# Mixer A of both groups in one pipeline with a new order of the projection blocks, and a prefix that transposes x in two halves

## The chip, the core and the metric

One core of a Trainium2 chip. Its engines are called TensorE (PE), VectorE (DVE), ScalarE (ACT), GpSimd (POOL) and SyncE (SP), which issues nearly all of the DMAs. The metric is the device time of one execution in microseconds; every time is counted from the first instruction of the execution unless it says otherwise.

## The reference, cut to what matters

A step through two layers of a hybrid backbone, for 128 context tokens and 1024 latent tokens, with width 1024. The change lies in the even layer, ahead of its recurrence:

```python
def even_layer(x, shift, scale, gate, ...):
    h = rms_norm(x, norm_pre) * (1.0 + scale) + shift      # shift, scale = silu(c) @ ada_w + ada_b
    qa, ka, va, ga, pb, gb = split_cols(h @ w_in, ...)
    # mixer A: 8 query heads in 2 groups of 4, one key/value head each
    #   context tokens: softmax over the context tokens, with a sink
    #   latent tokens, in blocks of 128: softmax over 128 cached keys and the blocks t-1, t, t+1
    ya = gqa_context(qa, ka, va, sink) or gqa_window_latent(rope(qa), rope(ka), va, k_ctx, v_ctx, sink)
    yb = rwkv_mix(pb, state, ...)                          # mixer B: a scan over the tokens
    y = concat([ya * silu(ga), yb * silu(gb)]) @ w_out
    return x + gate * rms_norm(y, norm_post)
```

The second, odd layer (differential attention) comes after all that the change touches. All products are made from values split into two parts, `hi` and `lo`, with three matmuls for one: hi x hi, hi x lo, lo x hi.

## The kernel before

The 1152 tokens are 9 tiles of 128 (`NT`): tile 0 holds the context tokens, 1 to 8 the latent ones. The normalized and modulated x lies transposed in `hh` and `hl` (width in 8 blocks, `KT`, by 1152 tokens), in SBUF, until the end of the stage that is called the first here.

**Prefix** (in `hybrid_step`, from L675). `mod_chunks` loads four chunks of 512 columns of `ada_w`, two loads of 1 MB each in a ring of four buffers, and makes 16 rows of shift and scale of them: 8 matmuls, a copy, a transpose and a VectorE instruction for each (L289 to L303). The chunks 0 and 1 are the shift of the blocks 0 to 3 and 4 to 7, the chunks 2 and 3 the scale. Then x is loaded in three thirds of three tiles, and `normed` scales the rows (L324 to L334). `modulated` (L336) takes 3 thirds x 8 blocks: three transposes into one PSUM bank (L342), ScalarE's scale and shift into `hf` (L345), VectorE's cast into `hh` (L347) and its residual into `hl` (L348). The modulation rows and the transposes share one pool of four PSUM banks.

**Two streams of work** follow, zipped step by step by `run`. `transposed` goes through 21 blocks of 128 output columns, each in three thirds of 384 tokens (`proj_T`, 24 matmuls a third, L368 to L370): `a` and `g` blocks are gates (`gate_T`, with `silu2`, stored to `gaT` or `pbT`), `b` blocks are the inputs of mixer B (`b_block`: the padded row `bo`, the sum of the neighbours `bs` on GpSimd at L472, the mix `bm`, stored to `pbT`). Of the b blocks 4 to 7 (the keys) the squares go to `bs`, `norms` (L493) sums them by matmuls, spreads the result to `yb` (L498), and `scale` transposes `yb` (L508) and multiplies `bm` by it (L512), both put off by some steps through the list `later`. `bs` and `bm` have one buffer each. The weights of each block are loaded to `raw` (two buffers), rounded on ScalarE and their rest taken on GpSimd (L261 to L263).

The other stream is mixer A, one generator `a_group` for each of the two groups, one after the other. At step k it projects tile k (`project`, L354 to L356, rotary factors on VectorE and GpSimd), sums up the values of tile k - 2 (`values`: transposes of the probabilities at L632, value matmuls at L643 to L645, store at L652), turns tile k (`turn`) and makes the probabilities of tile k - 1 in two rounds of two heads (`probs`: score matmuls at L601, masks at L604, maximum at L608, exponentials at L614). The scores have one PSUM tile of two banks. The keys `kst`, the values `vh` and `vl` and the group's weights `wah`, `wal` have one buffer each and are allocated anew for the second group.

**The order on the engines** of all this, and of the first pieces of the RWKV stage (up to item -1 of its loop), is made by a scheduler that simulates the time (`tc.block(schedule_with_timeline_sim=True)`): every instruction has a place in the order in which the program emits it, and of those that are ready the one with the lowest place goes first; each engine then runs its list in order. The buffers of the RWKV stage (`low`, `lora` and the operand tiles `hb`, L885 to L905) take the room of the first stage's tiles.

Of the kernel before, what the change touches and what calls it, by code (L numbers as in the profile page):

```python
# [141 lines left out]
def hybrid_step(ctx: ExitStack, tc: tile.TileContext, I, O, stop=99):  # L142
# [315 lines left out]
    def b_block(i, w, later, pool, psum, p_tr, hh, hl, ind):  # L458
# [29 lines left out]
        yb = tl(pool, [P, 2 * NT, 64], "yb", bufs=1)  # L488
# [54 lines left out]
    def a_group(g, hh, hl, wp, rp, ap, psum, rope, idb, msk):  # L543
# [6 lines left out]
        kr, vr = tl(ap, [P, P], "kr"), tl(ap, [P, 64], "vr")  # L550
        SP.dma_start(kr, I["akT"][g])
        SP.dma_start(vr, I["av"][:, g])
        stack_split(kst[:, 0:P], kr)
        dup_split(vh[:, 0], vl[:, 0], vr)
        kp, vph, vpl = (tl(ap, [P, P], n, F32R) for n in ("kp", "vph", "vpl"))
        qks, qss, prs = {}, {}, {}

        def project(t):
            ps = tl(p_pr, [P, 512], "ps")
            proj_nat(ps, hh, hl, wh, wl, t, THIRD)  # L560
            qk = qks[t] = tl(ap, [P, 5, 2, 64], "qk", bufs=2)
# [7 lines left out]
            else:  # L569
                dup_split(vh[:, t], vl[:, t], ps[:, 320:384])  # L570

        def turn(t):
            qk = qks.pop(t)
            pq, pk = tl(p_tr, [P, 512], "pt"), tl(p_tr, [P, 512], "pt")
            PE.transpose(pk[:, :P], qk[:, 4].rearrange("p o d -> p (o d)"), ident)
            stack_split(kp if t == 0 else kst[:, P * t:P * t + P], pk[:, :P])
            for r in range(4):
                PE.transpose(pq[:, P * r:P * r + P], qk[:, r].rearrange("p o d -> p (o d)"), ident)
            qs = qss[t] = tl(ap, [P, 2, 512], "qs", F32R, bufs=2)
# [3 lines left out]
        def near(t):  # L583

            if t == 0:
                return [(0, kp)], [(vph, vpl)], []
            lo, hi = max(1, t - 1), min(8, t + 1)
            kv = [(vh[:, j], vl[:, j]) for j in [0] + list(range(lo, hi + 1))]
            return ([(0, kst[:, 0:P]), (P, kst[:, P * lo:P * hi + P])], kv,
                    ([(P, 0)] if t > 1 else []) + ([(P * len(kv) - P, 1)] if t < 8 else []))  # L590

        def probs(t, hp):
            runs, kv, masks = near(t)
            nk = P * len(kv)
            qs = qss[t]
# [16 lines left out]
            p = prs[t, hp] = tl(ap, [P, 2, 512], "p", bufs=2)  # L612
# [8 lines left out]
        def values(t):  # L621
            kv = near(t)[1]
            pr = [prs.pop((t, hp)) for hp in range(2)]
# [32 lines left out]
        for k in range(NT + 2):  # L656
            if k < NT:
                project(k)
                yield
            if 2 <= k:  # L660
                yield from values(k - 2)
            if k < NT:
                turn(k)
                yield
            if 1 <= k <= NT:
# [8 lines left out]
    blk.__enter__()  # L674
    with ExitStack() as ph1:  # L675
        hp = ph1.enter_context(space("hT0", 1))
        hh, hl = tl(hp, [P, KT, TOK], "hh", F32R), tl(hp, [P, KT, TOK], "hl", F32R)
        with ExitStack() as su:
            xp = su.enter_context(space("su", 2))
            ps = su.enter_context(space("psu", 4, space=PSUM, side="right"))  # L680
            ahead = []
            for j in range(4):
                for _ in mod_chunks(0, 4 * j, 4, xp, ps, "ps", lambda: tl(xp, [P, P], "mrow"), 4, ahead):
                    pass
            ahead.pop()()
            thirds = []
            for i in range(3):
# [4 lines left out]
                normed(thirds[i], xp)  # L692
            for i in range(3):
                modulated(i, thirds[i], xp, ps, hh, hl)
# [6 lines left out]
        left, right, rope = load_cst(bp, "left", "right", "rope")  # L701
# [6 lines left out]
        for i, n in enumerate((left, right)):  # L708
            VE.tensor_copy(msk[i], n)

        def mixer_a():
            for g in range(2):
                yield from a_group(g, hh, hl, wp, rp, ap, psum, rope, idb, msk)

# [1111 lines left out]
```

## Time and profile before

| | us |
|---|---|
| three runs | 2169.96, 2173.63, 2176.01 |
| median | 2173.63 |
| the profiled execution | 2174.75 |
| its span, first to last instruction | 2173.0 |

Busy over the whole span: PE 2004.3 us (92%), VectorE 1466.5 us (67%), ScalarE 1070.9 us (49%), GpSimd 668.4 us (31%). The stretch of the change is the first 590 us. A row of a stretch gives, after its length, the busy time and the number of instructions of each engine, the granted clock of PE as a share of 2.4 GHz, the mean busy share of the 16 DMA engines and their GB/s. PEld is the load of a matmul's stationary operand. A row of the order of time gives start, duration, engine, line, instruction, what it writes and reads, the number of merged instructions, and in brackets the idle time before it and what ended it.

### The profile page before, as it was taken

The numbers are of one execution on the slowest core, as the hardware profiler recorded it, in microseconds if no ns is written. First come the engines' busy times: TensorE is split into PE (matmuls) and PEld (weight loads), VectorE is DVE, ScalarE is ACT, GpSimd is POOL, SyncE is SP. The second block draws the span as 40 slices with busy tenths as digits, with TensorE's granted clock in tenths as the row PEclk, the third lists the DMA queues.
The fourth block names the chain that finished last, engine by engine and source line by source line (L and its number), as shares of the span: only waits on it lengthen the run. The fifth ranks groups of instructions, "written<-read, shape, count | busy, mean of one in ns | idle before, by whom it ended". The sixth has DMA issues, their size and how long they took to land. (4 is left out here: it accounts for less than half of the span.)

```text
span 2173.0 us, 40867 instructions
## 1 busy us (share of the span) xinstructions
PE 2004.3 (92%) x15258; PEld 1780.6 (82%) x15258; DVE 1466.5 (67%) x3650; ACT 1070.9 (49%) x2856; POOL 668.4 (31%) x933
## 2 busy tenths in 40 slices
PE   6899998999688898988998889999999999999998
PEld 4899997999566777776776779899999999898786
DVE  3445546544565686868648758778788888887867
ACT  3433343433345455555436555555555555555643
POOL 0222132221046555665405311321212222222204
PEclk9999999999888999999999999999999999999999
DMA  7321221311354454543466440100010010101315
GB/s 285 122 86 62 83 76 58 106 52 43 99 181 129 127 170 139 172 131 115 137 193 216 151 124 5 53 28 30 27 30 28 29 30 28 34 23 47 96 58 182
DMA packets 164935, 205.73 MB, mean 95 GB/s; under 512 B 16352, under 2 KB 107904, under 8 KB 164736
## 3 DMA queue, kind: packets, MB, share of 16 engines
q1 hardware_dynamic: 161872, 198.25, 28.9%
q10 hardware_dynamic: 2864, 4.85, 0.7%
q8 instruction: 121, 1.98, 0.4%
q14 instruction: 78, 0.64, 0.1%
HBM read 152.32 MB, written 50.74 MB: 93 GB/s over the span
## 5 line engine op out<-in xcount | busy, mean ns | idle before, releaser
L1501 ACT ACTIVATE p<-s,mx 128x384 f32<-128x384 f32 (+1 forms) x400 | 225.1, 572 | 127.8 <-DVE mx L1498 106.9
L1496 DVE TENSOR_REDUCE mc<-s 128x1 f32<-128x384 f32 x384 | 205.1, 552 | 29.2 <-PE s L1494 25.8
L354 PE MATMUL ps<-wch,hh 128*128 128x384 f32 x576 | 205.7, 358 | 7.5 <-DVE hh L1645 6.1
L1494 PE MATMUL s<-kst,qs 128*128 128x384 f32 x768 | 197.0, 355 | 11.6 <-ACT p L1501 11.0
L355 PE MATMUL ps<-wcl,hh 128*128 128x384 f32 x576 | 198.9, 345 | 4.5 <-POOL wcl L263 4.5
L356 PE MATMUL ps<-wch,hl 128*128 128x384 f32 x576 | 197.2, 342 | 2.1 <-DVE hl L1646 2.0
L401 POOL TENSOR_TENSOR q<-ropea,ropeb 128x256 f32<-128x256 f32 x56 | 43.1, 769 | 450.0 <-DVE ropeb L398 322.8
L368 PE MATMUL ps<-hh,wgh 128*128 128x384 f32 x504 | 174.7, 347 | 6.3 <-DVE bo L234 6.3
L369 PE MATMUL ps<-hl,wgh 128*128 128x384 f32 x504 | 173.8, 345 | 0.0
L370 PE MATMUL ps<-hh,wgl 128*128 128x384 f32 x504 | 172.9, 343 | 0.0
L263 POOL TENSOR_TENSOR wgl<-raw,wgh 128x1024 fp32r<-128x1024 f32 (+1 forms) x39 | 75.1, 1929 | 293.6 <-ACT wgh L262 278.2
L1494 PEld LDWEIGHTS s<-kst,qs 128*128 128x128 f32 x768 | 127.0, 189 | 29.6 <-ACT p L1501 20.9
L1031 POOL TENSOR_TENSOR tmp<-mp,rp 128x126 f32<-128x126 f32 (+22 forms) x279 | 132.1, 473 | 53.3 <-DVE mp L1024 28.3
L1033 POOL TENSOR_TENSOR rp<-rp,tmp 128x126 f32<-128x126 f32 (+22 forms) x279 | 127.7, 458 | 21.9
L1377 ACT CAST ah<-pt 128x512 fp32r<-128x512 f32 (+2 forms) x168 | 86.2, 534 | 81.8 <-PE pt L1532 79.5
L1378 DVE TENSOR_TENSOR al<-pt,ah 128x512 fp32r<-128x512 f32 (+2 forms) x168 | 100.8, 616 | 33.7 <-ACT ah L1377 32.3
L354 PEld LDWEIGHTS ps<-wch,hh 128*128 128x128 f32 x576 | 110.4, 192 | 13.3 <-issue 3.4
L355 PEld LDWEIGHTS ps<-wcl,hh 128*128 128x128 f32 x576 | 110.2, 191 | 7.6 <-POOL wcl L263 7.2
L356 PEld LDWEIGHTS ps<-wch,hl 128*128 128x128 f32 x576 | 109.8, 191 | 3.9 <-DVE hl L1646 3.8
L368 PEld LDWEIGHTS ps<-hh,wgh 128*128 128x128 f32 x504 | 96.4, 191 | 8.2 <-DVE bo L234 6.9
L1532 PE MATMUL pt<-cst,p 128*128 128x128 f32 x584 | 95.2, 277 | 5.7 <-DVE p L1514 4.7
L1514 DVE SCALAR_TENSOR_TENSOR p<-p,lr,p 128x1152 f32<-128x1152 f32 (+1 forms) x72 | 99.8, 1386 | 0.3
(462 smaller groups left out, 5676.8 us busy)
## 6 DMA issues: line engine op xcount, KB each, us to landing
hb<-pbT SPq DMA_DIRECT2D x90, 256.0 KB, 4.2
adaw<-in_ada_w_dram SPq DMA_DIRECT2D x64, 256.0 KB, 3.5
raw<-in_wc_dram SPq DMA_DIRECT2D x48, 256.0 KB, 2.8
adaw<-in_ada_w_dram SPq DMA_DIRECT2D x8, 1024.0 KB, 11.7
pbT<-bm SPq DMA_DIRECT2D x16, 512.0 KB, 2.7
low<-lowT SPq DMA_DIRECT2D x16, 512.0 KB, 4.9
raw<-in_wo_dram SPq DMA_DIRECT2D x32, 256.0 KB, 2.8
raw<-in_wpb_dram SPq DMA_DIRECT2D x13, 512.0 KB, 3.6
```

What stands on the lines that cost most here:

```text
L354: PE.matmul(ps[:, :n], hh[:, k, s], wh[:, k], start=k == 0, stop=False)
L355: PE.matmul(ps[:, :n], hh[:, k, s], wl[:, k], start=False, stop=False)
L356: PE.matmul(ps[:, :n], hl[:, k, s], wh[:, k], start=False, stop=k == KT - 1)
L368: PE.matmul(ps[:, :THIRD], wh[:, k], hh[:, k, s], start=k == 0, stop=False)
L369: PE.matmul(ps[:, :THIRD], wh[:, k], hl[:, k, s], start=False, stop=False)
L370: PE.matmul(ps[:, :THIRD], wl[:, k], hh[:, k, s], start=False, stop=k == KT - 1)
L1031: eng.tensor_tensor(tv, mp[:, j:j + 1, 0:j].to_broadcast([P, n, j]), rpb[:, t:16, j:j + 1].to_broadcast([P, n, j]), ALU.mult)
L1033: eng.tensor_tensor(rpb[:, t:16, 0:j], rpb[:, t:16, 0:j], tv, ALU.add)
L1378: VE.tensor_tensor(lo, src, hi.bitcast(F32), ALU.subtract)
L1494: PE.matmul(s[c][:, :w], qs[:, e, z], hd.kp[:, z] if own else hd.kst[:, z, w * c:w * c + w], start=e == 0, stop=e == 1)
L1496: VE.tensor_reduce(mc[:, c:c + 1] if nb > 1 else mx, s[c][:, :w], axis=AX.X, op=ALU.min)
L1501: AE.activation(e[:, w * c:w * c + w], s[c][:, :w], AF.Exp, scale=-1.0, bias=mx, accum_out=sums[:, z, c:c + 1])
```

## The change

- `modulated` takes the blocks to do as an argument. The prefix makes the chunks 0 and 2 (shift and scale of the blocks 0 to 3), loads and normalizes x, makes chunk 1, modulates blocks 0 to 3 of all thirds, makes chunk 3, and modulates blocks 4 to 7. The transposes have three PSUM banks of their own, the modulation rows three.
- `yb` is no tile of its own any more, it lies in the first columns of `s` (the tile `bs`).
- `a_group` becomes `mixer_a`, one generator for both groups with steps u from 0 to 17 (`g, t = divmod(u, NT)`). `kst`, `vh`, `vl` hold tiles 1 to 8 only and are allocated once; the keys and values of tile 0 (`own`) and of the cache (`cache`) have two buffers. The second group's weights and cached keys are begun right after the first group's last projection. The probabilities `p` have three buffers instead of two.
- `hurried` wraps mixer A: its instructions get a place in the scheduler's order that is 1000 ahead of where they are emitted.
- The order of the 21 blocks is a new one.
- The window masks are loaded into a `raw` tile instead of standing beside the rotary factors.

```diff
+    def hurried(work, n):
+        while True:
+            with tc.high_priority(n):
+                if next(work, 0) == 0:
+                    return
+            yield
...
-    def modulated(i, xs, pool, psum, hh, hl):
+    def modulated(i, ks, xs, pool, psum, hh, hl):
         s = slice(THIRD * i, THIRD * i + THIRD)
-        for k in range(KT):
+        for k in ks:
...
-        yb = tl(pool, [P, 2 * NT, 64], "yb", bufs=1)
+        yb = s[:, :TOK].rearrange("p (n t) -> p n t", t=64)
...
-    def a_group(g, hh, hl, wp, rp, ap, psum, rope, idb, msk):
+    def mixer_a(hh, hl, wp, rp, ap, psum, rope, idb, msk):
         p_pr, p_tr, p_s, p_o = psum
-        wh, wl = weights(wp, I["wa"][g], THIRD, "wa", rp, bufs=1)
-        kst = tl(ap, [P, TOK], "kst", F32R)
-        vh, vl = tl(ap, [P, NT, P], "vh", F32R), tl(ap, [P, NT, P], "vl", F32R)
...
+        kst = tl(ap, [P, TOK - P], "kst", F32R)
+        vh, vl = tl(ap, [P, NT - 1, P], "vh", F32R), tl(ap, [P, NT - 1, P], "vl", F32R)
+        own, cache, ws = {}, {}, {}
+        def begin(g):
+            ws[g] = weights(wp, I["wa"][g], THIRD, "wa", rp, bufs=1)
+            kr, vr = tl(ap, [P, P], "kr"), tl(ap, [P, 64], "vr")
+            SP.dma_start(kr, I["akT"][g])
+            SP.dma_start(vr, I["av"][:, g])
+            own[g], cache[g] = ([tl(ap, [P, P], n + e, F32R, bufs=2) for n in ("k", "vh", "vl")] for e in "pc")
+            stack_split(cache[g][0], kr)
+            dup_split(*cache[g][1:], vr)
+        def project(u):
+            g, t = divmod(u, NT)
+            if t == 0 and g not in ws:
+                begin(g)
...
+            if t == NT - 1 and g == 0:
+                begin(1)
...
-            p = prs[t, hp] = tl(ap, [P, 2, 512], "p", bufs=2)
+            p = prs[u, hp] = tl(ap, [P, 2, 512], "p", bufs=3)
...
-        for k in range(NT + 2):
-            if k < NT:
+        for k in range(2 * NT + 2):
+            if k < 2 * NT:
...
+    sys_blocks = "a0 a1 b4 a2 b5 a3 b6 g0 b7 g1 b0 b12 b8 b1 b2 b3 b9 b10 b11 g2 g3"
...
-            ps = su.enter_context(space("psu", 4, space=PSUM, side="right"))
...
+            pt = su.enter_context(space("psut", 3, space=PSUM, side="right"))
+            ps = su.enter_context(space("psu", 3, space=PSUM, side="right"))
...
+            chunks(0)
+            chunks(2)
+            third()
+            third()
+            third()
+            chunks(1)
             for i in range(3):
-                modulated(i, thirds[i], xp, ps, hh, hl)
+                modulated(i, range(4), thirds[i], xp, pt, hh, hl)
+            chunks(3)
+            for i in range(3):
+                modulated(i, range(4, KT), thirds[i], xp, pt, hh, hl)
...
-        blocks = [("a", 0), ("a", 1)] + [("b", i) for i in (4, 0, 5, 1, 6)] + [("a", 2), ("a", 3)] + [
-            ("b", i) for i in (7, 2, 3, 12, 8, 9, 10, 11)] + [("g", i) for i in range(4)]
+        blocks = [(n[0], int(n[1:])) for n in sys_blocks.split()]
         rest = transposed(blocks, wp, rp, bp, psum[0], psum[1], hh, hl, ind)
         run(some(rest, 7), 1, None, 1)
-        run(rest, 56, mixer_a(), 2 * (4 * NT + 2 * NT - 2))
+        run(rest, 56, hurried(mixer_a(hh, hl, wp, rp, ap, psum, rope, idb, msk), 1000), 12 * NT * 1)
```

## Rows read from the trace of the kernel before

**Rows 1.** The table of stretches. Columns: from and to, length, busy time and number of instructions of PE, PEld, VectorE, ScalarE and GpSimd, the granted clock, the DMA share and GB/s.

```profile
25.40:34.10 8.70, 0.01 (x1) 0.00 (x0) 8.23 (x20) 6.53 (x11) 2.91 (x2) 0.68 1.04 393
34.10:53.20 19.10, 18.29 (x138) 12.23 (x138) 8.09 (x24) 2.04 (x8) 2.21 (x1) 0.88 0.48 179
53.20:82.00 28.80, 23.73 (x147) 22.11 (x147) 21.37 (x56) 17.79 (x37) 0.00 (x0) 0.88 0.11 30
...
337.00:357.00 20.00, 12.88 (x78) 10.28 (x77) 14.77 (x41) 8.46 (x22) 1.53 (x1) 0.89 0.10 37
357.00:390.00 33.00, 32.70 (x184) 31.19 (x185) 19.23 (x36) 14.27 (x35) 8.42 (x8) 0.91 0.30 90
...
401.00:550.50 149.50, 149.50 (x910) 144.27 (x909) 73.25 (x156) 52.50 (x123) 35.60 (x22) 0.99 0.16 57
550.50:590.10 39.60, 26.81 (x122) 20.32 (x120) 21.93 (x53) 13.18 (x35) 2.16 (x8) 0.78 0.32 93
75.50:590.10 514.60, 488.78 (x2913) 464.50 (x2913) 253.24 (x574) 188.65 (x426) 121.02 (x88) 0.97 0.24 78
```

**Rows 2.** Order of time, PE alone, at places where it is full: the end of a projection, a round of scores and transposes near 544 us, two value matmuls near 577 us.

```profile
543.81 0.34 PE L369 MATMUL ps<-hl,wgh 128*128 128x384 f32 x1
...
544.16 0.73 PE L601 MATMUL s<-kst,qs 128*128 128x128 f32 x4
...
545.61 0.82 PE L632 MATMUL pt<-cst,p 128*128 128x128 f32 x6
...
577.07 0.40 PE L643 MATMUL po<-ph,vh 128*128 128x512 f32 x1
...
577.30 0.40 PE L644 MATMUL po<-ph,vl 128*128 128x512 f32 x1
```

**Rows 3.** Order of time in the prefix: the scaling of x, GpSimd's split of the first weights, the later modulation matmuls, the first transposes, and the last units up to the return of the projections.

```profile
25.59 2.07 DVE L334 TENSOR_SCALAR x<-x,rsy 128x1024 f32<-128x1024 f32 x3
...
29.95 4.17 DVE L334 TENSOR_SCALAR x<-x,rsy 128x1024 f32<-128x1024 f32 x3
...
31.19 5.12 POOL L263 TENSOR_TENSOR wgl<-raw,wgh 128x1024 fp32r<-128x1024 f32 x2 [30.74 <-ACT wgh L262]
...
34.17 1.86 PE L289 MATMUL ps<-adaw,sc 128*2 128x128 f32 x8 [8.76 <-DVE x L334]
...
38.54 2.08 DVE L334 TENSOR_SCALAR x<-x,rsy 128x1024 f32<-128x1024 f32 x3
...
53.19 2.10 PE L342 MATMUL ps<-cst,x 128*128 128x128 f32 x15
...
71.39 1.02 DVE L348 TENSOR_TENSOR hl<-hf,hh 128x384 fp32r<-128x384 f32 x2
...
73.04 1.02 DVE L348 TENSOR_TENSOR hl<-hf,hh 128x384 fp32r<-128x384 f32 x2
...
74.36 0.56 DVE L348 TENSOR_TENSOR hl<-hf,hh 128x384 fp32r<-128x384 f32 x1
...
75.58 0.69 PE L368 MATMUL ps<-hh,wgh 128*128 128x384 f32 x1 [4.98 <-DVE bo L234]
```

**Rows 4.** Order of time between the two groups of mixer A.

```profile
342.24 1.04 PE L601 MATMUL s<-kst,qs 128*128 128x128 f32 x4 [2.81 <-ACT p L614]
...
350.89 0.30 ACT L421 CAST kst<-kr 128x128 fp32r<-128x128 f32 x1 [1.15 <-PE s L601]
...
356.33 1.26 ACT L473 ACTIVATE bm<-bo,mu 128x1154 f32<-128x1154 f32 x1 [0.40 <-issue]
...
359.70 0.60 PE L368 MATMUL ps<-hh,wgh 128*128 128x384 f32 x1
```

**Rows 5.** Groups of PE's instructions by line from 337 to 357 us. Columns: line, engine, operation, what it writes and reads, shape, count, busy us, mean ns of one, idle us before them and what ended it.

```profile
L601 PE MATMUL s<-kst,qs 128*128 128x128 f32 (+2 forms) x24 | 4.9, 347 | 2.8 <-ACT p L614 2.8
L632 PE MATMUL pt<-cst,p 128*128 128x128 f32 x23 | 4.4, 323 | 4.0 <-DVE p L619 2.8 <-DVE bm L512 1.2
L643 PE MATMUL po<-ph,vh 128*128 128x512 f32 x4 | 1.9, 463 | 0.3 <-ACT ph L634 0.3
```

**Rows 6.** Order of time at the hand-over to the RWKV stage: the last projection matmul, the stage's first matmul, and the first load and the matmul of its second direction.

```profile
550.26 0.34 PE L370 MATMUL ps<-hh,wgl 128*128 128x384 f32 x1
...
590.08 1.14 PE L905 MATMUL py<-low,lora 128*128 128x512 f32 x4 [1.00 <-PE po L645]
...
591.25 0.53 SPq L891 DMA_DIRECT2D low<-lowT  x1
...
596.18 2.04 PE L905 MATMUL py<-low,lora 128*128 128x512 f32 x4 [4.96 <-DMA lora<-loraT]
```

**Rows 7.** Groups of PE's instructions by line from 550.5 to 590.1 us, columns as in rows 5.

```profile
L601 PE MATMUL s<-kst,qs 128*128 128x128 f32 (+2 forms) x32 | 8.8, 417 | 5.0 <-ACT p L614 5.0
L632 PE MATMUL pt<-cst,p 128*128 128x128 f32 x38 | 6.9, 321 | 3.2 <-DVE p L619 3.2
L643 PE MATMUL po<-ph,vh 128*128 128x512 f32 x11 | 5.7, 515 | 1.3 <-ACT ph L634 1.3
```

**Rows 8.** Two tables of the stretch from 100 to 180 us: of all instructions, and of line L354 alone (its columns are PE, PEld, the clock and the DMAs; 8 of its matmuls make one tile of mixer A's projection, with as many of L355 and L356).

```profile
100.00:180.00 80.00, 79.39 (x489) 77.62 (x488) 34.66 (x89) 30.61 (x69) 24.66 (x21) 1.00 0.32 108
...
100.00:180.00 80.00, 13.80 (x40) 7.52 (x40) 1.00 0.32 108
```

**Rows 9.** Who waited for whom from 60 to 590 us: the scores matmuls and the softmax that frees their PSUM tile. Columns: us in total, times, longest.

```profile
PE s L601 <- ACT p L614: 9.9, 5, 3.1
```

More of the change, by code (lines that the diff above doesn't have):

```diff
@@ L541, in transposed @@
                 f()
[L543 removed]
+    def mixer_a(hh, hl, wp, rp, ap, psum, rope, idb, msk):
         p_pr, p_tr, p_s, p_o = psum
[L547 to L558 removed]
+        kst = tl(ap, [P, TOK - P], "kst", F32R)
+        vh, vl = tl(ap, [P, NT - 1, P], "vh", F32R), tl(ap, [P, NT - 1, P], "vl", F32R)
+        own, cache, ws = {}, {}, {}
+        qks, qss, prs = {}, {}, {}
+        def begin(g):
[10 more added lines that the diff above has]
+                begin(g)
+            wh, wl = ws[g]
+            kp, vph, vpl = own[g]
             ps = tl(p_pr, [P, 512], "ps")
             proj_nat(ps, hh, hl, wh, wl, t, THIRD)
[L561 removed]
+            qk = qks[u] = tl(ap, [P, 5, 2, 64], "qk", bufs=2)
             rope_apply(ap, rope, ps, 5, None if t == 0 else t - 1, [qk])
@@ L619, in probs, with values @@
                 VE.tensor_scalar(p[:, r, :nk], p[:, r, :nk], li[:, r:r + 1], None, op0=ALU.mult)
-        def values(t):
-            kv = near(t)[1]
-            pr = [prs.pop((t, hp)) for hp in range(2)]
+        def values(u):
+            g, t = divmod(u, NT)
+            kv = near(u)[1]
+            pr = [prs.pop((u, hp)) for hp in range(2)]
             po = tl(p_o, [P, 512], "po")
@@ L661, in a_group @@
                 yield from values(k - 2)
-            if k < NT:
+            if k < 2 * NT:
                 turn(k)
                 yield
-            if 1 <= k <= NT:
+            if 1 <= k <= 2 * NT:
                 for hp in range(2):
@@ L679, in hybrid_step, with third @@
             xp = su.enter_context(space("su", 2))
-            ps = su.enter_context(space("psu", 4, space=PSUM, side="right"))
[L681 to L685, printed above, removed]
+            pt = su.enter_context(space("psut", 3, space=PSUM, side="right"))
+            ps = su.enter_context(space("psu", 3, space=PSUM, side="right"))
             thirds = []
-            for i in range(3):
+            def third():
+                i = len(thirds)
                 thirds.append([tl(xp, [P, D], "x", bufs=NT) for _ in range(3)])
@@ L692, in hybrid_step, with chunks @@
                 normed(thirds[i], xp)
+            def chunks(j):
+                ahead = []
+                for _ in mod_chunks(0, 4 * j, 4, xp, ps, "ps", lambda: tl(xp, [P, P], "mrow"), 4, ahead):
+                    pass
+                ahead.pop()()
+            chunks(0)
[4 more added lines that the diff above has]
+            chunks(1)
             for i in range(3):
-                modulated(i, thirds[i], xp, ps, hh, hl)
+                modulated(i, range(4), thirds[i], xp, pt, hh, hl)
+            chunks(3)
+            for i in range(3):
+                modulated(i, range(4, KT), thirds[i], xp, pt, hh, hl)
         ap = ph1.enter_context(space("ap", 1))
@@ L700, in hybrid_step @@
                 for n, b in (("ppr", 2), ("ptr", 3), ("psc", 1), ("ppo", 1))]
-        left, right, rope = load_cst(bp, "left", "right", "rope")
+        rope, = load_cst(bp, "rope")
         ind, = load_cst(rp, "ones")
@@ L707, in hybrid_step @@
         VE.tensor_copy(idb, ident)
[L708 to L713, printed above, removed]
-        blocks = [("a", 0), ("a", 1)] + [("b", i) for i in (4, 0, 5, 1, 6)] + [("a", 2), ("a", 3)] + [
-            ("b", i) for i in (7, 2, 3, 12, 8, 9, 10, 11)] + [("g", i) for i in range(4)]
+        sides = tl(rp, [P, 1024], "raw")
+        SP.dma_start(sides[:, :2 * P], I["cst"][:, CST["left"][0]:sum(CST["right"])])
+        for i in range(2):
+            VE.tensor_copy(msk[i], sides[:, P * i:P * i + P])
+        blocks = [(n[0], int(n[1:])) for n in sys_blocks.split()]
         rest = transposed(blocks, wp, rp, bp, psum[0], psum[1], hh, hl, ind)
         run(some(rest, 7), 1, None, 1)
-        run(rest, 56, mixer_a(), 2 * (4 * NT + 2 * NT - 2))
+        run(rest, 56, hurried(mixer_a(hh, hl, wp, rp, ap, psum, rope, idb, msk), 1000), 12 * NT * 1)
     if stop <= 1:
```

26 lines of the change are left out of this document (14 added, 12 removed).

## The prediction

> **What bounds the kernel now.** I read the table of stretches first, then the order of time at the places where it shows idle time, then the groups of matmuls in those places. Everything that the change touches lies in the first 590 us; what follows runs in its old order, so the question is how much earlier that part starts. From 401 to 550 us TensorE (PE) is busy for the whole 149.5 us at a granted clock of 0.99, so the stage is bound by the amount of matrix work, and time can only be won where PE runs dry. It does so in four stretches [rows 1]: 25.4 to 34.1 us (0.01 of 8.7 us busy), 53.2 to 82 us (23.73 of 28.8), 337 to 357 us (12.88 of 20) and 550.5 to 590.1 us (26.81 of 39.6, clock 0.78). Busy overstates there, because a busy matmul overlaps the next one; what the same instructions cost when PE is full has to be read from pitches.
>
> The pitches [rows 2]: a 384-column projection matmul takes PE 0.17 us (two of them from 543.81 to 544.16); one round of scores (two heads, with its mask matmuls) takes PE from 544.16 to 545.61, 1.45 us; six transposes last 0.82 us, about 0.11 us each after the first; a 512-column value matmul comes every 0.23 us (577.07 to 577.30).
>
> **Part 1, the prefix.** The diff moves the modulation columns of the first four blocks of x (shift and scale) to the front, and 12 of the 24 units of transposing and modulating (3 thirds of the tokens by 8 blocks) ahead of the last chunk of weights, with PSUM banks apart from those of the modulation rows. Nothing is added; the same loads are issued on SP, in the order chunk 0, chunk 2, x, chunk 1, chunk 3, and the later chunks still wait for the buffers of the earlier ones. Before, all 24 units stand behind the last modulation row: the first transposes come at 53.19, the last unit's residual at 74.36 for 0.56 us, and PE resumes at 75.58 after 4.98 us of idling [rows 3]. Two units take 1.65 us (from 71.39 to 73.04), 0.83 us each. Twelve units behind the last row instead of 24 are 12 x 0.83 = 10 us less. Against that stand 36 transposes x 0.11 = 4 us of PE among the modulation matmuls; some 1.3 us of it (12 transposes of the first third, scaled by 25.59 + 2.07 = 27.7) can fall into the gap that ends at 34.17, so 2.7 us are added. The third third of x is scaled only at 38.54 + 2.08 = 40.6 [rows 3], so its four units start then, and VectorE still has room (8.09 of 19.1 us busy from 34.1 to 53.2 [rows 1]) for about the 12 units' work (its subtractions alone are 1.02 us for two, and the pace of 0.83 us a unit makes 10 us in all). That is nearly an exact fit, with little slack. I take 10 - 2.7 = **-7 us**; bounds -3 (half of the units slip behind) and -10.
>
> VectorE's scaling of three x tiles takes 2.07 us alone and 4.17 us while GpSimd (POOL) splits the first weights, 31.19 for 5.12 us [rows 3]. The Trainium skill, page "SBUF — State Buffer", section "Who interferes with whom", says of this pair that a VectorE instruction with two SBUF inputs and a GpSimd one that reads SBUF exclude each other, and the later waits to the end of the other. It speaks against putting the first units there. By the row the second third is late by 2.1 us and is hidden; by the rule a unit could be held for both splits (rival 4).
>
> **Part 2, one pipeline.** Between the groups PE starves from 337 to 357 us. In the order of time the scores wait 2.81 us for the softmax of the round before, the second group's cached keys enter `kst` only at 350.89, the next b block's `bm` is begun at 356.33, and the projections resume at 359.70 [rows 4]. Two causes lie together: a new `kst`, `vh`, `vl` with one buffer each, so that the second group waits for the first one's last scores; and block b7 followed by b2, whose `bs`, `bm` wait for the norms of b7. The work there: 24 scores matmuls are 3 rounds, 4.4 us; 23 transposes x 0.11 = 2.5; 3 x 4 value matmuls x 0.23 = 2.8 [rows 5]; some 1.5 for the rest of the 78 instructions; 11 us, so 9 us are lost. From 357 to 390 the clock is 0.91 [rows 1], that is partly at the lower of its two levels after that gap: 33 x 0.09 = 3 us more. The change gives the keys and values of each group's own and cached tokens two buffers, leaves `kst` to be overwritten tile by tile, and puts a gate block behind each of b4 to b7. Sum **-12 us**, bounds -5 (the block chain remains) and -15 (the later hole near 400 goes too). `yb` now lies in `bs`: the next block's GpSimd addition (`bs`) waits for the transposes of `yb`, and POOL's queue behind it holds weight splits and the rotary additions. The block after has a gate's projection in between (3 x 24 x 0.17 = 12 us of PE), which covers it; without cover it costs 2 us per block, 8 at most. The second group's weights still have one buffer, and mixer A waits for them as before, beside projections.
>
> **Part 3, the tail.** The last projection matmul is at 550.26; then mixer A's last tiles run alone until the RWKV stage's first matmul at 590.08 [rows 6]. The work that is left: 32 scores matmuls are 4 rounds, 5.8 us; 38 transposes 4.2; 33 value matmuls 7.6; under 1 for the rest: 18.5 us [rows 7] of 39.6. The higher priority (1000 places in an order of some 4000 instructions, by the counts from 75.5 to 590.1 us [rows 1], so about a quarter of the stage) puts this work ahead of the last projections, which then end the stage dense. The 18.5 us remain, the other **-21 us** go; bounds -21 and -12 (the lead is used up in part by waits for the second group's weights and gates).
>
> **What is late next.** The RWKV operand tiles are put where `hh` lies, which the last projection now reads to the end of the stage. Before, they were loaded during the tail, and the first matmul followed mixer A by 1.0 us. Now these loads are exposed. The nearest rows: the second direction's loads begin at 591.25 and its matmul comes at 596.18, 4.9 us later [rows 6]. **+5 us**, bounds +1 and +10 (if the second direction is late by as much again). The new order itself: mixer A's steps come closer together than any stretch before shows. From 100 to 180 us it projected 5 tiles (40 matmuls of 8 per tile) with PE busy 79.39 of 80 us [rows 8], a pace of 16 us a tile instead of 28 later; but only the projections kept that pace. I take **+3 us**, with bounds -2 (cover of the many small holes) and +15.
>
> Sum: -7 - 12 - 21 + 5 + 3 = -32 us. The profiled execution took 2174.75 us (span 2173.0), so 2142.8; the median of the three runs shown is 1.1 us below it, so **2142 us**. All bounds together give 2127 and 2179.
>
> **Rivals.** (1) The priority does not carry mixer A past the last projections, as its waits for weights, gates and buffers eat the lead. Then parts 1 and 2 remain without the exposed loads: -19, with +3 for the order -16, 2158 us. For it: the second group's weights follow the first group's last projection. Against: a quarter of the stage is some 120 us, three times the tail. (2) Slower: PE takes its queue in order, so a score round put in front as early as it can go stops the projections behind it until the softmax of the round before is out of PSUM (there is one scores buffer). The price is the 2.81 us of [rows 4] for each of 36 rounds, 101 us: 2142 + 101 = 2243 us; it decides from 32 / 36 = 0.9 us a round. Against it: in the whole stretch from 60 to 590 us these waits add up to 9.9 us in five places [rows 9], and those I know lie in stretches with no projections to run. (3) All holes close, the small ones too, and the loads come early because the keys' and weights' room is free: -10 - 15 - 21 + 1 - 2 = -47, 2127 us or somewhat less. (4) The prefix gains nothing for the port: the first units hold the second and third scaling up by the 5.12 us of both splits [rows 3], so part 1 is -2 and the time 2147 us. That is the page's rule above at its full weight.
>
> **How the numbers follow.** Forecast 0.68 (2130 to 2156), rival 1 0.12, rival 2 0.06, rival 3 0.07, rival 4 0.07. Range: 2122 to 2164; below lies a part of rival 3, above rival 2 and the worst sums of the forecast, together under 0.2. A measurement can tell some 0.3%, 6.5 us, from no change. Faster by more than that 0.88; within it 0.06 (the upper bounds of parts 1 to 3 at once); slower 0.06 (rival 2).
>
> **What would show it.** Right: the last unit's `hl` near 67 us instead of 74.9; no gap of projections like that from 337 to 359.7; mixer A's last store some tens of us before the last projection matmul; that matmul near 553 us (550.3 - 7 - 12 + 18.5 + 3), and the RWKV stage's first matmul near 558 us (590.1 - 32), the distance from there to the end unchanged. Wrong: score rounds preceded by PE idling through the middle of the stage (rival 2); mixer A's last store still behind the last projection (rival 1); or a distance from the first RWKV matmul to the end that has grown, which would mean that the gain is given back in a stage that I hold to be only shifted.

## The result, and the profile after

The changed kernel took 2146.1 us (median of four runs, 2142.95 to 2149.89) beside 2174.82 us for the kernel before on the same chip: a ratio of 0.9871, with a 95% interval from 0.9843 to 0.9898. The forecast was 2142 us. The profiled execution took 2148.68 us, its span 2146.9 us, against 2174.75 and 2173.0 before, so 26.1 us less, where the sum said 32.

The lines of the kernel have moved a little: the first matmul of a projection step is now L376 (its three are L376 to L378), scores are L622, the softmax's `p` is L635, transposes of `p` L654, value matmuls L665 to L667, the RWKV stage's first matmul L939.

First the table of stretches of the changed kernel, columns as in rows 1. The first four answer to [rows 1] at the same clock times; the stage ends earlier, so the dense stretch and the tail have their own bounds.

```profile
25.40:34.10 8.70, 5.07 (x24) 3.44 (x24) 8.49 (x30) 8.68 (x20) 0.56 (x1) 0.85 1.04 388
53.20:82.00 28.80, 25.54 (x156) 22.99 (x154) 14.44 (x39) 12.90 (x28) 2.41 (x1) 0.94 0.27 84
337.00:357.00 20.00, 18.12 (x109) 16.57 (x107) 12.72 (x33) 8.45 (x26) 1.11 (x2) 1.00 0.45 125
357.00:390.00 33.00, 32.44 (x198) 31.63 (x199) 16.85 (x35) 14.61 (x32) 12.36 (x12) 1.00 0.33 103
401.00:537.70 136.70, 136.05 (x829) 129.98 (x828) 68.44 (x136) 51.33 (x117) 29.13 (x20) 1.00 0.14 48
537.70:561.40 23.70, 16.66 (x83) 12.44 (x82) 14.83 (x37) 8.58 (x24) 2.71 (x8) 0.86 0.46 145
```

The hole between the groups is filled: from 337 to 357 us PE is busy 18.12 us instead of 12.88, and the 33 us behind it run at a clock of 1.00 instead of 0.91. The tail is there still, 23.7 us instead of 39.6, and 7 us of it are idle.

Now the order of time at the places that the prediction named: the end of the prefix, the last projection, and the hand-over to the RWKV stage. They answer to [rows 3] and [rows 6].

```profile
67.19 1.02 DVE L356 TENSOR_TENSOR hl<-hf,hh 128x384 fp32r<-128x384 f32 x2
...
69.13 0.69 PE L376 MATMUL ps<-hh,wgh 128*128 128x384 f32 x1 [3.12 <-DVE bo L242]
...
537.69 0.34 PE L378 MATMUL ps<-hh,wgl 128*128 128x384 f32 x1
...
538.46 0.59 SPq L925 DMA_DIRECT2D low<-lowT  x1
...
561.37 0.39 ACTq L674 DMA_DIRECT2D yT<-gt  x1
...
561.43 1.17 PE L939 MATMUL py<-low,lora 128*128 128x512 f32 x4 [1.00 <-PE po L667]
...
567.56 0.77 PE L939 MATMUL py<-low,lora 128*128 128x512 f32 x1 [4.96 <-DMA lora<-loraT]
```

The last `hl` units begin at 67.19 and 67.66 (74.36 before), and the projections resume at 69.13 (75.58). The last projection matmul comes at 537.69, but mixer A's last store comes at 561.37, 24 us behind it and not ahead of it. The operand loads of the RWKV stage (`low`) are issued right after the last projection and land during the tail, as before; its first matmul follows mixer A by 1.00 us, as before.

So the first RWKV matmul is 28.65 us earlier (590.08 to 561.43), in three parts: 6.45 us at the end of the prefix; 6.1 us between there and the last projection (550.26 - 75.58 = 474.7 us before, 537.69 - 69.13 = 468.6 us now); 16.1 us in the tail (39.8 to 23.7). From the first RWKV matmul to the end the profile shows 1585.5 us against 1582.9, so 2.6 us of it are not seen in the span.

### The profile page after: what moved, and what is told of

Read it like the earlier page. It is cut to its first block, busy times and chain, and to the rows that moved or that the text cites. A ratio compares the mean times of both kernels' runs of the same rounds, so it can differ in the third digit from the quotient of the medians.

```text
span 2146.9 us, 40860 instructions
## 1 busy us (share of the span) xinstructions
PE 1995.7 (93%) x15258; PEld 1775.3 (83%) x15258; DVE 1453.5 (68%) x3650; ACT 1069.4 (50%) x2856; POOL 665.7 (31%) x933
## 5 line engine op out<-in xcount | busy, mean ns | idle before, releaser
L376 PE MATMUL ps<-hh,wgh 128*128 128x384 f32 x504 | 174.5, 346 | 5.8 <-DVE bo L242 4.0
L378 PE MATMUL ps<-hh,wgl 128*128 128x384 f32 x504 | 171.5, 340 | 0.0
L376 PEld LDWEIGHTS ps<-hh,wgh 128*128 128x128 f32 x504 | 95.5, 189 | 7.8 <-DVE bo L242 4.6
L271 POOL TENSOR_TENSOR wcl<-raw,wch 128x512 fp32r<-128x512 f32 x54 | 72.8, 1358 | 83.3 <-ACT wch L270 83.3
```

The lines of the kernel that those rows point to most:

```text
L271: eng.tensor_tensor(lo[:, j:j + w], raw[:, :w], hi[:, j:j + w].bitcast(F32), ALU.subtract)
L376: PE.matmul(ps[:, :THIRD], wh[:, k], hh[:, k, s], start=k == 0, stop=False)
L378: PE.matmul(ps[:, :THIRD], wl[:, k], hh[:, k, s], start=False, stop=k == KT - 1)
```

## The experiments

Each time stands beside runs of the kernel before on the same chip; that kernel's median was 2169.7 to 2176.5 us on them, so the ratios are what is compared. "Last step" is the start of the last projection step, "first RWKV" that of the RWKV stage's first matmul, both in the profiled execution. Each place is read from one execution, so how far it moves between executions of one kernel is not known.

| kernel | median us | ratio, 95% interval | last step | first RWKV |
|---|---|---|---|---|
| before | 2174.8 | 1 | 549.9 | 590.1 |
| changed | 2146.1 | 0.9871 (0.9843 to 0.9898) | 537.4 | 561.4 |
| prefix only | 2170.9 | 0.9981 (0.9964 to 0.9998) | 545.5 | 581.2 |
| prefix and block order | 2166.8 | 0.9957 (0.9938 to 0.9976) | 545.0 | 581.2 |
| changed, old block order | 2150.7 | 0.9883 (0.9846 to 0.9921) | 545.4 | 567.3 |
| changed, no priority | 2154.7 | 0.9911 (0.9882 to 0.9940) | 527.9 | 570.5 |
| steps 1.25 times, priority | 2171.0 | 0.9979 (0.9962 to 0.9996) | 548.4 | 580.1 |
| steps 1.25 times, no priority | 2152.8 | 0.9918 (0.9888 to 0.9948) | 546.3 | 574.9 |
| steps 1.6 times | 2159.3 | 0.9934 (0.9908 to 0.9959) | 564.9 | 572.7 |
| steps twice | 2203.4 | 1.0141 (1.0113 to 1.0169) | 609.1 | 616.6 |
| 111 steps | 2144.9 | 0.9863 (0.9835 to 0.9891) | 545.1 | 556.6 |
| 114 steps | 2150.2 | 0.9882 (0.9853 to 0.9910) | 542.7 | 566.5 |
| `p` in two buffers | 2161.6 | 0.9924 (0.9895 to 0.9952) | 547.1 | 572.8 |
| the same, room kept | 2145.8 | 0.9867 (0.9846 to 0.9888) | 537.8 | 564.5 |

**The prefix alone.** The kernel before with the prefix's part of the diff (chunks 0, 2, x, 1, 3; units in two halves; own PSUM banks).

> The kernel before with the new prefix alone. My prediction's part 1: 2174.8 - 7 = 2168 us, the last hl unit near 67.7 us instead of 74.4, and the distance from there to the first RWKV matmul as before (515 us). The rival: the 6.5 us are given back at the gap between the two groups or in the tail, where mixer A's chain and not PE sets the end: 2172 to 2175 us with the first RWKV matmul at 587 us or later.

2170.9 us, a ratio of 0.9981: 4 us, with an interval from 0.4 to 8, which leaves room for both forecasts. In its profile (2163.03 us, the fastest of ten executions) the last `hl` comes at 71.16, 3.2 us earlier than before and not 6.7, and the first RWKV matmul 8.8 us earlier. So by the places the gain is not given back at the gap or in the tail, and the rival falls. That the gain grows from 3.2 to 8.8 us, 4.5 of it in a tail that this edit does not touch, shows how far a stage can shift with an edit elsewhere; why it did here was not tried. Why the last `hl` is 3.5 us later than in the changed kernel is seen in SP's queue, first of the changed kernel, then of this one, with GpSimd and VectorE:

```profile
21.11 0.33 SPq L269 DMA_DIRECT2D raw<-in_wga_dram  x1
23.65 5.84 SPq L293 DMA_DIRECT2D adaw<-in_ada_w_dram  x4
36.17 0.34 SPq L269 DMA_DIRECT2D raw<-in_wga_dram  x1
```

```profile
20.00 1.61 SPq L261 DMA_DIRECT2D raw<-in_wga_dram  x2
22.62 8.07 SPq L285 DMA_DIRECT2D adaw<-in_ada_w_dram  x4
...
34.45 4.92 POOL L263 TENSOR_TENSOR wgl<-raw,wgh 128x1024 fp32r<-128x1024 f32 x2 [34.01 <-ACT wgh L262]
...
34.77 2.32 DVE L240 TENSOR_SCALAR rsy<-rst 128x3 int32<-128x3 int32 x1
37.12 2.26 DVE L242 TENSOR_TENSOR rst<-rsy 128x3 f32<-128x3 f32 x1
```

The changed kernel loads its masks into one of the two `raw` buffers, so that the second half of the first weights (512 KB) is sent behind the last modulation weights. Here it is sent ahead of them, on queues that move some 390 GB/s in this stretch [rows 1]: 512 KB are 1.3 us, and the first scaling of x begins 0.9 us later (25.53 instead of 24.61). With both halves there, GpSimd splits them one behind the other, 4.92 us, and VectorE is held twice, by 2.32 and 2.26 us on instructions that take 0.16 or 0.17 us alone, the second until 39.38, where the second split ends (39.37); in the changed kernel the second split comes only at 45.45, and VectorE is held once (rows in the part on the prefix below). The third scaling of x so begins at 42.76 instead of 39.73, 3.0 us later, which is most of the 3.5. With the new block order alone the weights are loaded as here, and both splits again follow each other (4.91 us).

**Which part closes the gap between the groups.** Two runs: the changed kernel with the block order of before, and the kernel with the new prefix given only the new block order.

```diff
-    sys_blocks = "a0 a1 b4 a2 b5 a3 b6 g0 b7 g1 b0 b12 b8 b1 b2 b3 b9 b10 b11 g2 g3"
+    sys_blocks = "a0 a1 b4 b0 b5 b1 b6 a2 a3 b7 b2 b3 b12 b8 b9 b10 b11 g0 g1 g2 g3"
```

> The changed kernel with the block order of before (b4 b0 b5 b1 b6 a2 a3 b7 b2 b3 b12 b8 to b11, gates last), one pipeline for both groups as changed. My prediction's part 2 named two causes of the gap at 337 to 357 us. If the pipeline alone closes it, 2144 to 2150 us. If the block order does (b7 followed by b2, whose bs and bm wait for the norms of b7; and bs now also holds yb, 2 us for each of four blocks without a gate block as cover), 5 to 10 us come back: 2151 to 2157 us, with a stretch of little PE work where b7 meets b2.

> The kernel before with the new prefix and the new block order, but still two groups one after the other at the ordinary priority. If the pipeline is what closes the gap, the gap between the groups stays and the time is that of the prefix alone, 2168 to 2173 us. If the block order closes it, 2158 to 2164 us.

With the pipeline (and its priority) in the old order the first RWKV matmul comes at 567.3, 13.9 us earlier than with the prefix alone; the new order then adds 5.9 us (2.6 us in the medians by ratio, within their intervals). With the order alone it comes at 581.2, where the prefix alone has it. The stretches show it, first of the kernel with the order alone, then of the one with the pipeline and the old order:

```profile
357.00:390.00 33.00, 25.49 (x150) 23.15 (x149) 20.07 (x47) 11.70 (x36) 3.93 (x6) 0.90 0.16 57
```

```profile
337.00:357.00 20.00, 18.32 (x118) 16.26 (x118) 15.73 (x45) 9.69 (x27) 2.36 (x4) 1.00 0.16 56
```

The new order only moves the hole to some 20 us later: 7.5 us idle at a clock of 0.90. The pipeline fills it in either order, and without the priority too (the next run has PE busy for all of 337 to 357 us). The time of the order alone, 2166.8, falls between what the two theories gave, and by the ratios it is 5 us less than that of the prefix alone, for which the two traces show no place; so it is the hole that is still there, and not the time, that decides between the theories.

**The priority.** The changed kernel with `mixer_a` not wrapped.

```diff
-        run(rest, 56, hurried(mixer_a(hh, hl, wp, rp, ap, psum, rope, idb, msk), 1000), 12 * NT * 1)
+        run(rest, 56, mixer_a(hh, hl, wp, rp, ap, psum, rope, idb, msk), 12 * NT * 1)
```

> The changed kernel with mixer A's steps at the ordinary priority; all else as changed. The priority's theory: it is what shortened the end of the mixer stage (23.7 us from the last projection to the first RWKV matmul, 39.6 before), so without it about 16 us come back: about 2162 us. The other theory, order of emission: mixer A and the blocks take PSUM tiles (ps, pt) and the raw tiles from shared rings in the order in which the program asks for them, so a priority can't pass it by more than a step; the tail got shorter because the two groups run as one pipeline: 2143 to 2151 us, with the last projection some 0 to 5 us earlier and the tail longer by as much.

2154.7 us: between the two theories, and neither number holds. The tail is 3 us longer than before the change; its row:

```profile
527.90:570.50 42.60, 28.62 (x142) 22.11 (x141) 24.77 (x60) 14.56 (x40) 2.71 (x8) 0.80 0.30 87
```

Beside the changed kernel's tail that is 28.62 us of work instead of 16.66. The priority carries about 12 us of mixer A's work ahead of the last projections, not the 26.8 that stand in the tail of before, and it is worth 9 us here, in the ratios as in the place of the first RWKV matmul (570.5 and 561.4).

**Handing mixer A out sooner.** If a priority can't carry it past the last projections, the order in which the program asks for its tiles can: mixer A's 108 steps are handed out twice as fast against the block steps, then 1.6 times (`12 * NT * 8 // 5`).

```diff
-        run(rest, 56, hurried(mixer_a(...), 1000), 12 * NT * 1)
+        run(rest, 56, hurried(mixer_a(...), 1000), 12 * NT * 2)
```

> The changed kernel, but mixer A's steps are handed out twice as fast against the block steps, so that all of them are emitted by half of the rest. Order of emission: mixer A's last value matmul then comes some 98 steps of three projection matmuls (50 us) ahead of the last projection; the tail's idle 7 us and the lower clock in it (0.86 for 16.7 busy us, 2.3 us) go, the loads of the RWKV operands are exposed (+5): about 2142 us. If instead mixer A's own chain sets its pace on the chip, PE waits in front of its score rounds, up to 2.8 us for each of about 20 rounds that come closer together: up to 2190 us. If the priority alone had ruled the order, emission would change nothing: 2146 us.

> As the run with steps twice as fast, but 1.6 times, so that mixer A's last value matmul falls just about at the last projections. Order of emission: the tail's 7 us of idling and 2.3 us of clock go, the loads cost up to 5 us, and the rounds are less crowded than at twice: 2137 to 2142 us. If mixer A's chain sets the pace: PE waits up to 1.5 us for each of 20 rounds, up to 2170 us.

Both are slower than the changed kernel, by 57 us and 13 us, so the first theory falls for the time, though it is right on the place: mixer A's last store then comes at 561.5 (last step 609.1) and, with 1.6 times, at 567.5 (last step 564.9). Two costs came up. The first is the one that the prediction feared and then did not see. The kernel with steps twice as fast, the row of 450 to 530 us, and below it, in order of time, two score rounds, with what ScalarE did ahead of the second, and the first RWKV matmul:

```profile
450.00:530.00 80.00, 65.38 (x354) 60.12 (x354) 40.04 (x77) 33.61 (x69) 19.88 (x19) 0.85 0.30 97
```

```profile
455.66 0.48 PE L622 MATMUL s<-kc,qs 128*128 128x128 f32 x1 [4.32 <-ACT p L635]
...
493.53 1.15 ACT L429 CAST bs<-bo 128x1152 fp32r<-128x1152 f32 x1 [6.11 <-DMA bo<-pbT]
494.58 0.68 ACT L635 ACTIVATE p<-s,mx 128x512 f32<-128x512 f32 x1
...
496.08 0.47 PE L622 MATMUL s<-kc,qs 128*128 128x128 f32 x1 [6.49 <-DVE bs L430]
...
616.59 0.76 PE L939 MATMUL py<-low,lora 128*128 128x512 f32 x1 [6.77 <-DMA lora<-loraT]
```

And who waited for whom on PE from 69 to 530 us in the same kernel (us in total, times, longest):

```profile
PE ps L376 <- DVE vl L435: 11.9, 6, 3.9
PE s L622 <- ACT p L635: 6.7, 2, 4.3
PE s L622 <- DVE bs L430: 6.5, 1, 6.5
PE ps L376 <- DVE bo L242: 5.4, 3, 3.1
```

The score rounds wait for the softmax (6.7 us) and once, 6.5 us, for what the view puts down to VectorE's half of a split `bs`, which ends at 496.06. ScalarE stood 6.11 us at its half of the same split, whose input is a DMA; the exponentials that free the score tile were behind it in the queue and ended 0.1 us before VectorE's half, so the round would have waited for the softmax nearly as long. More is lost where the projections wait for their two PSUM tiles (`ps`), which VectorE evicts late: `vl` of mixer A's own projection (11.9 us) and `bo` of a gate (5.4 us). The granted clock is 0.85 in this stretch, 1.00 in the changed kernel's dense one. The second cost is the exposed loads: with no tail the first RWKV matmul waits 6.77 us for `lora`, and comes 7.5 us after the last projection step (7.8 us with 1.6 times).

**A little sooner.** Is there a lowest point between?

> The changed kernel with mixer A's steps handed out 1.25 times as fast (1.6 times gave 2159 us, twice 2203 us, once 2146 us). If the pace costs in proportion from the start, about 2151 us (a quarter of the way to 1.6 is 0.42 of 13 us). If the lowest point lies between, because part of the 23.7 us tail goes while the operand loads (7 us in the two runs without a tail) still hide behind what is left of it, 2138 to 2143 us.

> The changed kernel with mixer A's steps handed out 111 instead of 108 to the 56 of the rest. In the program's order of PE instructions the last but two tiles' values then stand ahead of 42 and 5 of the 504 projection steps, the last one's behind all of them (changed kernel: 18, 0, 0). Tail's theory: the work of one tile more goes into the dense stage, the tail falls from 23.7 us to 10 to 16 us, its idling by 4 to 7 us, and the operand loads (7 us) stay hidden: 2139 to 2144 us. If what rules is how the steps happen to interleave with the blocks' evictions on ScalarE and VectorE (1.25 times gave 2171 us, 1.6 times 2159 us), any small change is worth up to +-15 us: 2150 to 2165 us.

> The same with 114 steps; in the program's order the last but two tiles' values stand ahead of 11, 0 and 0 projection steps, nearly as in the changed kernel. Tail's theory: 2145 to 2150 us, as the changed kernel. Interleaving: 2150 to 2165 us.

The edits are `12 * NT * 5 // 4`, `111` and `114` in the place of `12 * NT * 1`. 111 steps give 2144.9 us, a ratio of 0.9863, which is the changed kernel's within the measurement; 114 give 2150.2, 1.25 times give 2171.0. The tail's theory is right on the mechanism with 111 steps: from the last step to the first RWKV matmul it is 11.5 us instead of 24.1, and that matmul comes 4.9 us earlier than in the changed kernel. But the second direction's first matmul then follows 9.6 us later instead of 6.1: its loads had been hidden by the tail too. With 114 steps the time lies where the two theories meet; the tail is 23.8 us, as the tail's theory said, but the last step comes 5.4 us later than in the changed kernel. At 1.25 times both forecasts are wrong, by 20 us and more. The time is not smooth in the pace, and not monotone: 2146, 2145, 2150, 2171, 2159, 2203 for 108, 111, 114, 135, 172 and 216 steps. At 1.25 times the first RWKV matmul is 18.7 us later than in the changed kernel: the last step comes 11.1 us later, and the tail, with 31.7 us, is 7.6 us longer. PE's waits from 69 to 530 us are 17.5 us in all, against 9.2. One such place, in order of time:

```profile
398.18 1.15 ACT L429 CAST bs<-bo 128x1152 fp32r<-128x1152 f32 x1 [4.39 <-DMA bo<-pbT]
...
400.83 0.10 POOL L470 MEMSET bo<- 128x2 f32 x1 [5.95 <-DVE bs L430]
...
400.96 0.27 ACT L475 COPY bo<-ps 128x128 f32<-128x128 f32 x1 [1.63 <-POOL bo L471]
401.12 0.76 ACT L476 COPY bo<-ps 128x256 f32<-128x256 f32 x2
...
401.55 0.69 PE L376 MATMUL ps<-hh,wgh 128*128 128x384 f32 x1 [2.97 <-ACT bo L476]
```

ScalarE stands 4.39 us at a split whose input is still on its way from DRAM; behind it in its queue are the copies that free a projection's PSUM tile. The first of them waits 1.63 us more, for GpSimd to clear the edge of a new `bo`, which in turn waits for VectorE's half of the split; PE stops for 2.97 us. The changed kernel has the same wait at 352.22 (3.57 us), where mixer A's work fills most of it.

> The run with steps 1.25 times as fast (2171 us), without the raised priority. Its loss beside the changed kernel stood in projections that waited for PSUM tiles whose evictions by ScalarE and VectorE came late (13.3 us in ten waits from 69 to 530 us) and in a tail of 31.7 us. If the raised priority puts mixer A's work on those two engines ahead of the evictions, these waits go without it: 2150 to 2160 us. If the faster steps alone do it, 2165 to 2180 us. If the priority is worth as much as at the ordinary pace (9 us), 2180 us.

2152.8 us. Without the priority the time is as the first theory said, by the ratios 13 us less. But the profiles put only 5.2 us of the 17 between them ahead of the first RWKV matmul (580.1 and 574.9), and 12 behind it, in code that the edit does not touch. The first part is where the theory has it: the projections' waits for evictions fell from 13.8 to 9.1 us. ScalarE's wait for the split is still there (4.42 us, to 394.41), and PE stops for 1.81 us instead of 2.97. For the other part, which is not shown to be the priority's, see the last section. At the ordinary pace the priority wins 9 us, at 1.25 times it loses 5 at the first RWKV matmul: it is no term with a size of its own.

**The third buffer of `p`,** to which the prediction gave no term.

```diff
-            p = prs[u, hp] = tl(ap, [P, 2, 512], "p", bufs=3)
+            p = prs[u, hp] = tl(ap, [P, 2, 512], "p", bufs=2)
```

> The changed kernel with two buffers instead of three for p (the probabilities of one score round). My prediction gave the third buffer no term. If that is right, 2143 to 2149 us. If the third buffer lets a score round run ahead of the values that still read the two before, its lack costs 0.5 to 1 us for each of 16 tiles: 2152 to 2162 us.

> As the run with two buffers for p, which took 2162 us, but the 4 KB per partition that the third buffer held are given to an unused tile, so that the tiles after it lie where the changed kernel has them (left out of the changed kernel: nothing but the third buffer). In the run without it the first block's weights came only after the prefix (PE waits 10.2 us for them at 69 us; first projection at 69.99 instead of 33.56). Placement's theory: that was the whole loss, and the buffer is worth nothing: 2144 to 2150 us, first projection near 34 us. The buffer's theory: the prefix is repaired, but score rounds wait for the values: 2155 to 2162 us.

2161.6 us, 11.5 us more than the changed kernel by the ratios; and 2145.8 us once an unused tile of the third buffer's size gives the room back. The buffer is worth nothing that these runs can tell; the room that it takes, and with it most likely the place of the tiles behind it, is worth the 11 to 12 us. PE's waits from 30 to 120 us, of the kernel with two buffers:

```profile
PE ps L376 <- ACT wgh L270: 10.2, 1, 10.2
```

and its order of time, where the first weights are loaded:

```profile
65.12 1.67 SPq L269 DMA_DIRECT2D raw<-in_wga_dram  x2
68.89 1.04 ACT L270 CAST wgh<-raw 128x1024 fp32r<-128x1024 f32 x1 [2.08 <-DMA raw<-in_wga_dram]
...
69.99 0.69 PE L376 MATMUL ps<-hh,wgh 128*128 128x384 f32 x1 [10.19 <-ACT wgh L270]
```

The load of the weights is issued at the end of the prefix (65.12 instead of 21.11 us). In the changed kernel 48 projection matmuls, 8 us at the pitch of 0.17, run between 33.56 us and the end of the prefix; here none does, and the projections begin 0.9 us later than they resume there. With the room kept the load is issued at 21.31 and the first projection is at 35.00 again. That the weights' tiles, with 4 KB less per partition ahead of them, come to lie where the prefix still works is the reading that fits both runs; the traces do not show where a tile lies.

## Why the prediction was right, and where its sum was not

The forecast holds and the changed kernel is faster, but not by the way that was forecast. The sign that the prediction gave for rival 1, mixer A's last store still behind the last projection, is there, and the last projection matmul comes at 537.69 and not near 553. By its own steps, from 2142.8 to the profiled 2148.68 us:

**Part 1, the prefix: -7 forecast, -6.45 measured** (75.58 to 69.13). The size holds. One step was overlooked: "the same loads are issued on SP" leaves out that the masks now go through `raw`, which changes the order of two loads and parts the two splits on GpSimd. With the prefix alone, where this is missing, the last `hl` is only 3.2 us earlier, next to the bound of -3; that 7 came out is in part owed to a step that the sum did not have. Rival 4 has its mechanism: its price is there for both splits with the prefix alone, and for one in the changed kernel. In order of time of the changed kernel:

```profile
27.24 0.17 DVE L248 TENSOR_SCALAR rsy<-rst 128x3 int32<-128x3 int32 x1
...
33.54 2.60 POOL L271 TENSOR_TENSOR wgl<-raw,wgh 128x1024 fp32r<-128x1024 f32 x1 [33.10 <-ACT wgh L270]
...
33.84 2.32 DVE L248 TENSOR_SCALAR rsy<-rst 128x3 int32<-128x3 int32 x1
```

The same instruction on three numbers a partition takes 0.17 us alone and 2.32 us when it starts behind a GpSimd split, until that ends (36.14 and 36.16). It costs 2.1 us here, and the twelve units are still done by 48.9, ahead of the last modulation row. The Trainium skill, page "SBUF — State Buffer", section "Who interferes with whom", has the instruction that comes later wait for the whole of the other; this row agrees on that. It names two SBUF inputs, or a mode with two ports, as the condition; this instruction has one input, and no run here shows its mode.

**Part 2, one pipeline, and the new order: -12 and +3 forecast, -12.1 measured together.** By the prices of the prediction (1.45 us a score round, 0.11 a transpose, 0.23 a value matmul) the tail now holds 3 rounds, 28 transposes and 21 value matmuls, 4.35 + 3.1 + 4.8, with under 0.5 for the rest 12.5 us, where 18.5 stood before. So the stage ahead of it holds 6 us more work and is still 6.1 us shorter. The +3 for the new order didn't come at this pace: beside the old order the new one is 5.9 us earlier at the first RWKV matmul. Steps that come closer together still do cost, at 1.25 times 18.7 us there (561.43 to 580.14), beyond the bound of +15. Of the two causes that the prediction laid together only one is a cause: the pipeline closes the gap in either block order, the block order alone doesn't.

**Part 3, the tail: -21 forecast, -9.9 measured.** Here the step failed that "puts this work ahead of the last projections, which then end the stage dense". The tail's loss fell from 39.6 - 18.5 = 21.1 to 23.7 - 12.5 = 11.2 us. Rival 1 had this mechanism with a tail left whole; half of it is what happened. Why the lead of 1000 places isn't used: faster steps move mixer A to the front (its last store 48 us ahead of the last step at twice the pace), with the same priority. So what holds it at pace 1 is the order in which the program hands out its steps. That a shared ring of tiles, `ps` or `pt`, is the very thing was argued and not tried.

**The exposed loads: +5 forecast, 0 measured,** because the tail that remains hides them. The price itself was right in kind and small in size: 7.5 and 7.8 us where there is no tail. The two errors belong together, and the prediction could have seen it: a tail with 21 us of loss hides some 7 us of loads for the first direction and some more for the second, so that ending it altogether is worth 11.2 - 7.5 = 4 us more, not 11; the run with 111 steps is 4.9 us ahead at the first matmul, 1.4 at the second direction's first one, and 4.5 at the end of its span. None of the kernels tried beats the changed one by more than these runs can tell.

**The distance to the end: unchanged forecast, +2.6 us measured,** within what it varies by in these runs (last section).

Together: +0.5 (part 1), -3.1 (part 2 with the order), +11.1 (part 3), -5 (loads), +2.6 (behind it), 6 us. Large errors of opposite sign, part 3 against the loads and the new order, leave a forecast that is 4 us off. That the kernel is faster was forecast by a mechanism that parts 1 and 2 bear out; that the number is so close is luck.

**Rival 2,** the slower one, was rightly put low at this pace: the score rounds' waits for the softmax are 4.3 us in two places from 60 to 590 us, where [rows 9] had 9.9. At twice the pace the kernel is slower than before by 1.4%, by this mechanism in part: 6.7 us of PE's waits are for the softmax, 13.2 with the one behind the split, and some 26 us are of projections that wait for evictions, which the rival didn't name.

## What to carry to other kernels

Before a tail is counted as gain, ask what is hidden behind it: loads that start when it starts keep most of their price when it goes. A priority did not move the work here as far as its number of places promised, and handing the steps out sooner did; work that comes closer together is paid for where ScalarE and VectorE free PSUM tiles late, a term that the rows of the slower kernel hardly show. When two splits or loads change their order, ask which small instructions they now hold up. When a buffer is added or removed, look at the first load of the tiles that lie behind it: their place, not the buffer, may be what the time shows.

## What the runs showed of the hardware

Two instances of the same item of the RWKV stage, one row of the kernel before and one of the changed kernel, with the same 652 matmuls:

```profile
821.13:873.61 52.48, 46.15 (x652) 37.58 (x652) 34.05 (x70) 27.12 (x71) 31.69 (x66) 0.93 0.43 127
```

```profile
797.98:847.50 49.52, 44.58 (x652) 37.37 (x652) 33.93 (x70) 27.07 (x71) 31.78 (x67) 0.97 0.45 134
```

The work of the other engines is the same to 0.2 us; the granted clock is 0.93 in one and 0.97 in the other, and 3 us lie between them, of which PE's own busy time is 1.6. In both the clock falls once to the lower of its two levels (0.50), at different places; the stretches, of the kernel before and of the changed one:

```profile
857.89:864.71 6.82, 6.82 (x89) 4.83 (x88) 1.93 (x5) 2.84 (x9) 0.00 (x0) 0.50 0.04 13
```

```profile
813.11:816.52 3.41, 3.41 (x16) 3.12 (x14) 1.18 (x4) 2.41 (x8) 2.94 (x7) 0.50 0.79 241
```

In the 10 to 11 us ahead of each PE is busy much alike, 9.04 of 10.89 us and 8.12 of 10.11, at a clock of 1.00. Over the fourteen profiles this item takes either 49.5 to 49.6 us, with the low stretch 15 us into it, or 52.4 to 52.5 us, with the low stretch 36 to 37 us into it, and nothing between. What decides between the two stays open.

The distance from the first RWKV matmul to the end comes out between 1573.2 us (1.25 times, no priority) and 1588.4 us (the old block order), in code that none of the edits touches. This item does not make that spread: the kernel with 1573.2 us has it in its longer form, and the mean granted clock over the distance is 0.97 there as in the changed kernel with 1585.5. What the spread is made of stays open too. So two spans that differ by less than these 15 us say little by themselves; a difference between two kernels here is read from the place of an event ahead of this stage, and from medians.
